# Memory attention of an encoder block: transposing the probabilities by halves of 64 query rows, into a PSUM tile of two banks

## The chip, the cores and the metric

The kernel runs on one core of a Trainium2 chip. The metric is the device time of one execution in microseconds (us). The kernel before takes 1399.69 us, the median of three runs (1399.4 to 1401.97).

## The reference, cut to what matters

The program is one encoder block on `x` of 1024 tokens by 1024 channels, in float32. Three mixers (dilated window attention "a", grouped-query attention "b", cross-attention into a memory of 256 tokens "m") are computed from one normalised input, gated, projected and merged. The change lies in the third mixer:

```python
kvm = rms_norm(mem, g_mem[layer]) @ w_mem_kv[layer]
km = kvm[..., :M_Q].reshape(b, n_mem, M_HEADS, M_HEAD_DIM)      # 256 keys, 4 heads of 128
vm = kvm[..., M_Q:].reshape(b, n_mem, M_HEADS, M_HEAD_DIM)
sm = jnp.einsum('bshd,bnhd->bhsn', mq.reshape(b, s, M_HEADS, M_HEAD_DIM), km).astype(jnp.float32)
pm = jax.nn.softmax(sm * (M_HEAD_DIM ** -0.5), axis=-1).astype(dt)
om = jnp.einsum('bhsn,bnhd->bshd', pm, vm).reshape(b, s, M_Q)
```

So for each of 4 heads there is a 1024 x 256 matrix of probabilities `pm` (queries by keys), and a product of it with 256 x 128 values.

## The kernel before, in words

Most products are made in float32r: each operand is split into a high and a low part (`split`, lines 106 to 108: ScalarE copies the high part, VectorE subtracts it from the source), and three products high-high, high-low and low-high are summed in PSUM. The kernel walks through stages: a start with keys, values and the memory's projections; the memory attention, together with the queries of mixer "b"; the attention of "b"; the long projections of mixer "a"; its window attention; the merge and the output projection.

The stage of the change runs from about 100 to 217 us. Its TensorE work is written out in an order by hand: `weave` takes steps of two generators in turn. One gives dense work from a queue (`b_q`, lines 301 to 305, matmuls with 256 moving columns; `mq_unit` and `add_gate`, lines 145 to 149, matmuls with 512 moving columns). The other is `m_att(h)`, the attention of one memory head. The order of the other engines' instructions is chosen by a scheduler; TensorE keeps the written order. The calls at the end of the stage are one `weave(1)` with dense work alone (the first `b_q`), then two queue items woven with head 0, two with head 1, one with head 2 and one with head 3.

`m_att(h)` works through its 1024 queries in four groups n of 256, as two tiles j of 128 query rows. In one step of its loop come `scores(n)`, then `trans(n - 2)`, then `pv(n - 3)`:

- `scores` (lines 579 to 595): six matmuls (line 127) into one PSUM bank, the row minimum on VectorE (line 586), its scaling (587), two exponentials on ScalarE (589), a reciprocal (592) and two scalings on VectorE (594). The result is the tile `pm`: 128 query rows by 2 j by 256 keys.
- `trans` (lines 597 to 606): four TensorE transposes (line 602), one for each tile j of queries and each half kt of the keys. A transpose is a matmul whose loaded weights are a 128 x 128 block of `pm` and whose moving operand is the 128 x 128 identity `ident`, a slice of the tile `cs`; so the profile names it `tr<-cs,pm`. All four land in one PSUM bank `tr`, from `pst()`, of which there are two in turn. Then `split` makes `mph` (ScalarE, line 107) and `mpl` (VectorE, line 108) from it, and the bank is free for the next but one group when `mpl` has been made.
- `pv` (lines 608 to 617): six matmuls (line 127, `ov<-mph,vmh` and so on) from `mph`, `mpl` and the values into a PSUM bank `ov`, a copy on ScalarE (616) and a DMA.

PSUM has eight banks. Two, named `d`, belong to the dense work for the whole program. The other six are given to each stage by `phase_psum(name, s2, s1, t, o)`: `s2` tiles of two banks (`pss()`), `s1` tiles of one bank (`pss1()`), `t` tiles of one bank for transposes (`pst()`), and `o` tiles for outputs (`pso()`). The start and the memory attention share one such opening, `phase_psum("ps_m", s1=3, t=2, o=1)`. Then comes `ps_b` for the attention of "b". `late` is a list of left-over pieces of the start that use `pst()`; `mq_unit` and `add_kv` take from it.

Some stages far behind the change run TensorE on parts of its 128 x 128 array, which the profile shows as rows*columns behind the operands' names: `64*128` (line 1589, scores of mixer "a" with a head dimension of 64: two heads, one on rows 0 to 63 and one on rows 64 to 127, into different banks), `64*64` (lines 1582 and 1654) and `128*64` (lines 821 and 1661). These are float32 matmuls, and the trace has two rows for each of them in the program. The transposes have one row each.

Of the kernel before, what the change touches and what calls it, by code (L numbers as in the profile page):

```python
# [50 lines left out]
def block(ctx: ExitStack, tc: tile.TileContext, x, xT, memT, cst, msk, bcst, tabA, gpost,  # L51
          wu, wv, wb, wmem, wbr, wout, out):
    nc = tc.nc
    V, A, G, PE = nc.vector, nc.scalar, nc.gpsimd, nc.tensor
# [12 lines left out]
    def phase_psum(name, s2=0, s1=0, t=0, o=0):  # L67
        assert 2 * s2 + s1 + t + o <= 6
        bank["n"] = (s2, s1, t, o)
        bank["i"] = 0  # L70
        bank["pool"] = tc.tile_pool(name=name, bufs=1, space=bass.MemoryType.PSUM, reuse_waits="tile")
        bank["p"] = bank["pool"].__enter__()

    def end_psum():
        bank["pool"].__exit__(None, None, None)

    def pss():
        return bank["p"].tile([P, 2, 512], F32, name="sc", tag="s2", bufs=bank["n"][0])

    def pss1():  # L80
        return bank["p"].tile([P, 512], F32, name="s1", tag="s1", bufs=bank["n"][1])

    def pst():
        bank["i"] += 1
        return bank["p"].tile([P, 4, 128], F32, name="tr", tag="t", bufs=bank["n"][2])

    def pso():
        return bank["p"].tile([P, 512], F32, name="ov", tag="o", bufs=bank["n"][3])
# [5 lines left out]
    ident = cs[:, C_ID:C_ID + 128]  # L94
# [11 lines left out]
    def split(dst_h, dst_l, src):  # L106
        A.activation(dst_h, src, AF.Copy)  # L107
        V.tensor_tensor(dst_l, src, dst_h.bitcast(F32), op=OP.subtract)  # L108
# [3 lines left out]
    def load_w(src, n=1024):  # L112
        if extra:
            extra.append(extra.pop(0))
        raw = (extra[0] if extra else wp).tile([P, 1024], F32, name="wr", bufs=WR)
        nc.sync.dma_start(raw[:, :n], src)
        wh = wp.tile([P, 1024], R, name="wh")
        wl = wp.tile([P, 1024], R, name="wl")
        split(wh[:, :n], wl[:, :n], raw[:, :n])
        k = n // 128  # L120
        return (wh[:, :n].rearrange("p (k f) -> p k f", k=k),
                wl[:, :n].rearrange("p (k f) -> p k f", k=k))

    def passes(out_ps, terms):
        n = len(terms)
        for i, (a, b) in enumerate(terms):
            PE.matmul(out_ps, a, b, start=i == 0, stop=i == n - 1)
# [37 lines left out]
    def run_items(count):  # L165
        for _ in range(count):
            n = done[0]
            prepare(n)
            prepare(n + 1)
            yield from queue[n][1](ready.pop(n))  # L170
            done[0] += 1

    def cost_items(count):
        return sum(q[2] for q in queue[done[0]:done[0] + count])
# [3 lines left out]
    def weave(count, att=None, att_cost=0.0, lead=1.0, prio=ATT_PRIO):  # L178
        dg = run_items(count)
        dc = cost_items(count)  # L180
        d = a = 0.0
        steps = 0
        live_d, live_a = True, att is not None
        while live_d or live_a:
            if live_d and (not live_a or a / att_cost >= min(1.0, d / dc * lead)):
                try:
                    d += next(dg)
                    steps += 1
                    if pend and steps % pace[0] == 0:
                        pend.pop(0)()  # L190
                except StopIteration:
                    live_d = False
                    d = 1e18
            else:
                try:
                    with tc.high_priority(offset=prio):
                        a += next(att)
                except StopIteration:
                    live_a = False
# [128 lines left out]
    kt = []  # L328
# [18 lines left out]
    late = []  # L347
# [102 lines left out]
    for k in range(8):  # L450
        if k % 2 == 0:
            load_wkv(k // 2)
        for e in range(2 if k == 0 else 1):
            t = slice(e * 512, e * 512 + 512) if k == 0 else slice(0, S)
# [29 lines left out]
    for c in range(2):  # L484
        t = st.tile([P, 4, 256], F32, name=f"mt{c}", tag=f"xk{c}")
# [86 lines left out]
    def m_att(h):  # L572
        qh, ql = MQ[h]
        for _ in range(4):
            yield 250
        st = {}

        def scores(n):
            sv = pss1().rearrange("p (t k) -> p t k", t=2)
            nm = mt_.tile([P, 2], F32, name="mnm", bufs=3)  # L580
            l = mt_.tile([P, 2], F32, name="mls", bufs=3)
            pm = mt_.tile([P, 2, 256], F32, name="pm", bufs=2)
            for j in range(2):
                t = slice((2 * n + j) * 128, (2 * n + j) * 128 + 128)
                passes(sv[:, j], [(qh[:, t], kmh[:, h]), (qh[:, t], kml[:, h]), (ql[:, t], kmh[:, h])])
            V.tensor_reduce(nm, sv, axis=AX.X, op=OP.min)
            V.tensor_tensor(nm, nm, rcol[:, 2 * n:2 * n + 2], op=OP.mult)
            for j in range(2):
                A.activation(pm[:, j], sv[:, j], AF.Exp, scale=nrcol[:, 2 * n + j:2 * n + j + 1], bias=nm[:, j:j + 1],
                             accum_out=l[:, j:j + 1])  # L590
            rl = mt_.tile([P, 2], F32, name="mrl", bufs=4)
            V.reciprocal(rl, l)
            for j in range(2):
                fp["mv"] = V.tensor_scalar(pm[:, j], pm[:, j], rl[:, j:j + 1], None, op0=OP.mult)
            st[n] = pm

        def trans(n):
            pm = st[n]
            tp = pst().rearrange("p (k t) q -> p k t q", k=2)
            for kt in range(2):  # L600
                for j in range(2):
                    PE.transpose(tp[:, kt, j, :], pm[:, j, kt * 128:kt * 128 + 128], ident)
            ph = mt_.tile([P, 2, 256], R, name="mph", bufs=2)
            pl = mt_.tile([P, 2, 256], R, name="mpl", bufs=2)
            split(ph, pl, tp.rearrange("p k t q -> p k (t q)"))
            st[n] = (ph, pl)

        def pv(n):
            ph, pl = st.pop(n)
            o = pso()  # L610
            terms = []
            for kt in range(2):
                terms += [(vmh[:, kt, h], ph[:, kt]), (vmh[:, kt, h], pl[:, kt]), (vml[:, kt, h], ph[:, kt])]
            passes(o[:, 0:256], terms)
            om = mt_.tile([P, 256], F32, name="om", bufs=2)
            A.activation(om, o[:, 0:256], AF.Copy)
            nc.sync.dma_start(od[2, h, :, n * 256:n * 256 + 256], om)

        for n in range(7):
            if n < 4:  # L620
                scores(n)
            yield 654
            if 0 <= n - 2 < 4:
                trans(n - 2)
            yield 436
            if 0 <= n - 3 < 4:
                pv(n - 3)
            yield 654
# [45 lines left out]
    add_gate(2, 2)  # L674
    early[len(queue)] = lambda: load_w(wu[U_G + 11])
    weave(1)
    weave(2, m_att(0), M_COST, 1.2)
    weave(2, m_att(1), M_COST, 1.2)
    weave(1, m_att(2), M_COST, 1.0)
# [548 lines left out]
    for n in range(28):  # L1228
        i, k = divmod(n, 4)
# [17 lines left out]
        for stage in (2, 1, 0):  # L1247
            r, at = divmod(n - 6 - (0, 2, 3)[stage], 3)
# [28 lines left out]
    for n in range(28):  # L1277
        i, k = divmod(n, 4)
# [5 lines left out]
        for j in range(4):  # L1284
            c = slice(j * 128, j * 128 + 128)
# [187 lines left out]
    r = RV[last, 0, 1]  # L1473
# [595 lines left out]
    s1 = [t[:, x] for t in [wp.tile([P, 1024], F32, name="wr", bufs=WR) for _ in range(2)] for x in half]  # L2069
# [127 lines left out]
    q, r = ss[7], ss[7][:, 3:4]  # L2197
# [148 lines left out]
```

## Time and profile before

| what | value |
|---|---|
| median of three runs | 1399.69 us (1399.4 to 1401.97) |
| the profiled execution, its own time | 1401.0 us |
| its span, from the first to the last instruction | 1399.2 us |
| mean granted TensorE clock | 0.997 |
| busy: TensorE, VectorE, ScalarE, GpSimd | 98%, 73%, 47%, 41% of the span |

"PE" is TensorE's matmuls, "PEld" its weight loads, DVE is VectorE, ACT ScalarE, POOL GpSimd, SP the engine that issues DMAs. In a timeline each row gives the start in us, the time in us, engine, line, operation, output tile and operand tiles, TensorE rows*columns, the shape of the moving operand and the number of instructions merged into the row. A matmul's time runs until its results are out, so the times of successive matmuls overlap; how fast they follow each other is read from the starts.

### The profile page before, as it was taken

To read this page: it belongs to the slowest core of one execution; us is meant where nothing else is said; L and a number is where in the kernel's file an instruction comes from. 1 tells how busy PE (TensorE), PEld (TensorE's weight loads), DVE (VectorE), ACT (ScalarE), POOL (GpSimd) and SP (SyncE) were. 2 spreads that over 40 slices of the span, in tenths; PEclk is the share of its full clock that TensorE was granted. 3 is DMA by queue.
4 is the path that set the end of the run, shared out by engine and by line. 5 is a ranking of instruction groups with operands and counts; after the bars stand their busy time and mean duration, and the time that the engine had idled before them with its cause. 6 is when DMAs were issued, how large, how long until landed. Compare 5 with 4: busy or idle time off the path is not lost.

```text
span 1399.2 us, 21844 instructions
## 1 busy us (share of the span) xinstructions
PE 1375.7 (98%) x7775; PEld 1105.8 (79%) x7775; DVE 1019.9 (73%) x1824; ACT 658.5 (47%) x1384; POOL 579.9 (41%) x444
## 2 busy tenths in 40 slices
PE   7999999999999999999999999999999999999997
PEld 7799986666666789988888888888887787778886
DVE  7768667776776597776777776677776566668977
ACT  6544455656655345333333333333336666653332
POOL 0507702675666000245555554355651243552003
PEclk9999999999999999999999999999999999999999
DMA  6356522322243688424323333333337676876455
GB/s 233 105 181 209 187 102 98 102 83 84 80 142 127 221 258 253 139 83 134 98 93 106 120 112 114 106 121 119 114 121 266 193 197 191 254 189 214 147 193 180
DMA packets 121933, 212.30 MB, mean 152 GB/s; under 512 B 32512, under 2 KB 61024, under 8 KB 121824
## 3 DMA queue, kind: packets, MB, share of 16 engines
q1 hardware_dynamic: 112512, 196.98, 44.0%
q10 hardware_dynamic: 9312, 13.93, 2.7%
q8 instruction: 61, 1.00, 0.3%
q14 instruction: 48, 0.39, 0.1%
HBM read 144.48 MB, written 66.38 MB: 151 GB/s over the span
## 4 chain that ended last, share of the span: by engine, by line
PE 89%; DVE 3%; POOL 2%; DMA 2%; ACT 2%; issue 1%; SPq 0%; DVEq 0%; POOLq 0%; ACTq 0%
PE s L1326 35%; PE d L1891 6%; PE s L1236 4%; PE s L2115 4%; PE ov L821 3%; PE sc L2033 3%; PE s L1287 3%; PE d L147 3%; PE d L145 3%; PE d L149 3%; PE s L1589 2%; PE tr L1661 2%; PE tr L787 2%; PE s L806 2%; PE s L805 2%; PE d L2115 2%
## 5 line engine op out<-in xcount | busy, mean ns | idle before, releaser
L812 POOL TENSOR_TENSOR bl<-bl,bp 128x512 f32<-128x512 f32 x96 | 133.1, 1386 | 54.2 <-ACT bp L808 48.7
L1326 PE MATMUL s<-hh,vS 128*128 128x512 f32 x400 | 133.4, 395 | 0.0
L1326 PE MATMUL s<-vA,vS 128*128 128x512 f32 x450 | 106.6, 390 | 0.0
L108 DVE TENSOR_TENSOR vS<-vot,vS 128x512 fp32r<-128x512 f32 x75 | 86.4, 1153 | 19.9 <-ACT vS L107 19.9
L1601 DVE CUSTOM_DVE_ANT_0 pra<-s,mask 128x192 f32<-128x192 f32 (+2 forms) x192 | 52.8, 327 | 63.8 <-PE s L1589 35.9
L1326 PEld LDWEIGHTS s<-vA,vS 128*128 128x128 f32 x450 | 84.5, 188 | 18.3
L808 ACT ACTIVATE bp<-s 128x512 f32<-128x512 f32 x128 | 75.6, 595 | 43.3 <-PE s L806 42.3
L788 DVE TENSOR_REDUCE bn<-tr 128x1 f32<-128x512 f32 x128 | 84.9, 683 | 12.9 <-PE tr L787 11.7
L145 PE MATMUL d<-hh,wh 128*128 128x512 f32 x224 | 89.3, 399 | 2.4 <-DVE fth L218 2.4
L1602 ACT ACTIVATE pra<-pra,sts 128x192 f32<-128x192 f32 (+2 forms) x176 | 75.2, 430 | 31.5 <-DVE sts L1601 31.4
L149 PE MATMUL d<-hh,wl 128*128 128x512 f32 x224 | 89.4, 399 | 0.0
L1326 PEld LDWEIGHTS s<-hh,vS 128*128 128x128 f32 x400 | 75.3, 188 | 17.7
L147 PE MATMUL d<-hl,wh 128*128 128x512 f32 x224 | 88.8, 397 | 0.0
L1326 PE MATMUL s<-hl,vS 128*128 128x512 f32 x200 | 79.1, 395 | 0.0
L1326 PE MATMUL s<-hh,wh 128*128 128x512 f32 x200 | 78.4, 392 | 0.0
L1326 PE MATMUL s<-hh,wl 128*128 128x512 f32 x200 | 78.4, 392 | 0.0
L1326 PE MATMUL s<-hl,wh 128*128 128x512 f32 x200 | 77.8, 389 | 0.0
L1330 ACT ACTIVATE vv<-s 128x512 f32<-128x512 f32 x50 | 29.9, 598 | 85.8 <-PE s L1326 59.3
L1070 POOL TENSOR_TENSOR vot<-wr 128x512 f32<-128x512 f32 x13 | 22.2, 1707 | 111.7 <-DVE vv L1206 111.7
L821 PE MATMUL ov<-bp,VS 128*64 128x512 f32 x256 | 58.5, 599 | 0.0
L1070 POOL TENSOR_TENSOR vot<-vot,vA 128x512 f32<-128x512 f32 x12 | 19.3, 1608 | 90.8 <-DVE vS L108 90.8
L145 PEld LDWEIGHTS d<-hh,wh 128*128 128x128 f32 x224 | 42.2, 188 | 16.2 <-issue 5.5
(629 smaller groups left out, 4050.9 us busy)
## 6 DMA issues: line engine op xcount, KB each, us to landing
wr<-in_wu SPq DMA_DIRECT2D x40, 512.0 KB
vA<-in_wu SPq DMA_DIRECT2D x24, 512.0 KB
qkd<-ko SPq DMA_DIRECT2D x96, 128.0 KB
wl<-thd SPq DMA_DIRECT2D x24, 512.0 KB
wos<-os SPq DMA_DIRECT2D x12, 512.0 KB
wr<-in_wbr SPq DMA_DIRECT2D x24, 256.0 KB
aq<-qkd SPq DMA_DIRECT2D x12, 512.0 KB
ak<-qkd SPq DMA_DIRECT2D x12, 512.0 KB
```

Source lines behind the costliest of these rows:

```text
L108: V.tensor_tensor(dst_l, src, dst_h.bitcast(F32), op=OP.subtract)
L145: PE.matmul(dst, wh[:, k, :], hh[k][:, t], start=k == 0, stop=False)
L147: PE.matmul(dst, wh[:, k, :], hl[k][:, t], start=False, stop=False)
L149: PE.matmul(dst, wl[:, k, :], hh[k][:, t], start=False, stop=k == 7)
L788: fp["last"] = V.tensor_reduce(st[i]["n"][:, j, c:c + 1], s, axis=AX.X, op=OP.min)
L808: A.activation(pp, s, AF.Exp, scale=-1.0)
L812: G.tensor_tensor(lsum[i % 2], lsum[i % 2], pp, op=OP.add)
L821: PE.matmul(o[e * 64:e * 64 + 64], VS[:, kt, kv], d.pop(kt), start=kt < 2, stop=kt >= NT - 2)
L1326: PE.matmul(BANK[n, c], a, b, start=k == 0 and q == 0 and not more, stop=k == 3 and q == 2, skip_group_check=c in "XW")
L1602: A.activation(src, src, AF.Exp, scale=-1.0, bias=bias, accum_out=sts[:, 1, h, T:T + 1])
L1891: PE.matmul(ps_, a, b, start=k == 0 and q == 0, stop=k == 3 and q == 2)
L2115: PE.matmul(dst[:, e[0]:e[1]], a, b, start=k == 0 and q == 0, stop=k == 3 and q == 2)
```

## The change

`trans` takes a tile of two banks from `pss()` in place of one bank from `pst()`. Each of the four transposes becomes two: one of query rows 0 to 63 (r = 0, rows 0 to 63 of TensorE, into the first bank) and one of query rows 64 to 127 (r = 1, rows 64 to 127, into the second bank), each with 64 x 128 probabilities as weights and a 64 x 64 identity as the moving operand. `split` reads the two banks in one instruction each and writes `mph` and `mpl` in the same order as before. For this the stage's PSUM is opened anew behind the first dense item: `ps_h` has one tile of two banks, three tiles `s1` and one tile `o`, six banks in all.

```diff
         def trans(n):
             pm = st[n]
-            tp = pst().rearrange("p (k t) q -> p k t q", k=2)
+            tp = pss()
             for kt in range(2):
                 for j in range(2):
-                    PE.transpose(tp[:, kt, j, :], pm[:, j, kt * 128:kt * 128 + 128], ident)
+                    for r in range(2):
+                        rs, c = slice(64 * r, 64 * r + 64), 128 * kt + 64 * j
+                        PE.transpose(tp[:, r, c:c + 64], pm[rs, j, kt * 128:kt * 128 + 128], ident[rs, rs])
             ph = mt_.tile([P, 2, 256], R, name="mph", bufs=2)
             pl = mt_.tile([P, 2, 256], R, name="mpl", bufs=2)
-            split(ph, pl, tp.rearrange("p k t q -> p k (t q)"))
+            split(*[z.rearrange("p k (t r q) -> p r (k t) q", t=2, r=2) for z in (ph, pl)],
+                  tp[:, :, 0:256].rearrange("p r (m q) -> p r m q", m=4))
             st[n] = (ph, pl)
@@
     early[len(queue)] = lambda: load_w(wu[U_G + 11])
     weave(1)
+    assert not late
+    end_psum()
+    phase_psum("ps_h", s2=1, s1=3, o=1)
     weave(2, m_att(0), M_COST, 1.2)
```

The transposes' line is 602 before and 604 after; later lines move by 3, and by 6 behind the new opening. There are now eight transposes in each of 16 groups (4 heads by 4 groups), and one tile for them in place of two in turn. On TensorE the order of everything else is as before. On VectorE and ScalarE the built program holds the same instructions, and for head 2 in a slightly other order; the DMA issues of that stage change places in a few spots.

## The prediction

> **What bounds the kernel now.** I read the page's busy shares first, then the stretch that holds the change, then its list of waits.
>
> ```profile
> PE 1375.7 (98%) x7775; PEld 1105.8 (79%) x7775; DVE 1019.9 (73%) x1824; ACT 658.5 (47%) x1384; POOL 579.9 (41%) x444
> PE 89%; DVE 3%; POOL 2%; DMA 2%; ACT 2%; issue 1%; SPq 0%; DVEq 0%; POOLq 0%; ACTq 0%
> ```
>
> TensorE is busy 98% of the span and makes 89% of the chain that ended last.
>
> ```profile
> 100.00:217.00 117.00, 117.00 (x817) 108.19 (x816) 83.72 (x203) 56.90 (x139) 54.08 (x81) 1.00 0.47 163
> ```
>
> This is the stage of the change: length, then busy time of TensorE, its weight loads, VectorE, ScalarE, GpSimd, then clock, DMA share and GB/s. TensorE works 117.00 of 117.00 us. In the list of waits from 100 to 240 us only one line is TensorE's, and it lies in the next stage:
>
> ```profile
> PE tr L787 <- DVE bn L788: 0.5, 1, 0.5
> ```
>
> So what the change adds to or takes from TensorE's sequence moves the end nearly one to one; what it does to the other engines counts only where TensorE comes to wait.
>
> **The transposes now.** Two groups in TensorE's timeline, the first among 256-column matmuls, the second among 512-column ones:
>
> ```profile
> 124.47 0.28 PE L303 MATMUL d<-wbh,hl 128*128 128x256 f32 x1
> 124.59 0.60 PE L602 MATMUL tr<-cs,pm 128*128 128x128 f32 x4
> 124.94 0.36 PE L305 MATMUL d<-wbl,hh 128*128 128x256 f32 x1
> 125.14 0.28 PE L301 MATMUL d<-wbh,hh 128*128 128x256 f32 x1
> 125.26 0.28 PE L303 MATMUL d<-wbh,hl 128*128 128x256 f32 x1
> ...
> 184.96 0.39 PE L145 MATMUL d<-hh,wh 128*128 128x512 f32 x1
> 185.19 0.60 PE L602 MATMUL tr<-cs,pm 128*128 128x128 f32 x4
> 185.55 0.48 PE L147 MATMUL d<-hl,wh 128*128 128x512 f32 x1
> 185.86 0.39 PE L149 MATMUL d<-hh,wl 128*128 128x512 f32 x1
> ```
>
> From the group's start to the second dense matmul behind it: 125.14 - 124.59 = 0.55 and 185.86 - 185.19 = 0.67 us. One step of dense work is in it (125.26 - 125.14 = 0.12; 185.19 - 184.96 = 0.23), so four transposes cost 0.43 to 0.44 us, 0.11 each, with no gap on either side. All 16 groups are thus 16 x 0.44 = 7.0 us, and no change to them can win more.
>
> **What is removed and added on TensorE.** No row before shows a half transpose in a series, so its price comes from other work on parts of the array, late in the kernel:
>
> ```profile
> 1068.81 0.40 PE L1891 MATMUL d<-hh,wh 128*128 128x512 f32 x1
> 1069.13 1.14 PE L1589 MATMUL s<-ak,aq 64*128 64x256 f32 x8
> 1070.20 0.50 PE L1891 MATMUL d<-hh,wh 128*128 128x512 f32 x1
> 1070.54 0.40 PE L1891 MATMUL d<-hl,wh 128*128 128x512 f32 x1
> 1070.78 0.40 PE L1891 MATMUL d<-hh,wh 128*128 128x512 f32 x1
> ...
> 1097.89 0.46 PE L1582 MATMUL s<-ak,aq 64*64 64x64 f32 x16
> 1098.28 0.76 PE L1628 MATMUL tr<-cs,pra 128*128 128x128 f32 x5
> ...
> 1109.83 1.15 PE L1654 MATMUL tr<-app,avs 64*64 64x64 f32 x32
> 1110.91 1.03 PE L1589 MATMUL s<-ak,aq 64*128 64x128 f32 x9
> ```
>
> Three things are read here.
>
> *Parts work side by side.* Line 1654 issues 32 matmuls of 64 moving columns, two at a time on different rows: 16 sets take 1110.91 - 1109.83 = 1.08 us. Line 1582 issues 16, four at a time: 4 sets take 0.39. If a set costs c and going in and out costs d, 16c + d = 1.08 and 4c + d = 0.39, so c = 0.058 and d = 0.16 us. Eight half transposes are four such sets: 4 x 0.058 + 0.16 = 0.39 us until the next dense matmul may start.
>
> *Going in costs.* Line 1589 starts 0.32 us behind a 512-column matmul that is followed after 0.24 otherwise (1070.78 - 1070.54): 0.08 to 0.09 us in which the array runs empty.
>
> *Coming out costs beyond d.* The first dense matmul behind takes until 1070.54 - 1070.20 = 0.34 in place of 0.24: 0.10 us, its weight load, which otherwise hides behind the matmul ahead.
>
> The Trainium skill, TensorEngine Tiling (Array Packing), Key Properties, says that changing the tiling mode, not just the tile, drains TensorE. The rows above agree (0.08 us on the way in). The Trainium skill's Theoretical Speedup on the same page gives up to 2x for a dimension of 64 or less; by that alone, an estimate, the 7.0 us would become 3.5.
>
> Sum for one group among 512-column work: 0.09 in + 0.39 + 0.34 = 0.82 us to the second dense matmul behind, against 0.67 now: +0.15. Among 256-column work the dense steps are 0.12 on both sides, so it is the same. 16 groups: +2.4 us.
>
> The weights of a half transpose are 128 columns wide, those of line 1654 64. Their loads:
>
> ```profile
> L602 PEld LDWEIGHTS tr<-cs,pm x64: 137/140/143, 110.3 to 211.9; 128*128 128x128 f32 x64
> L1654 PEld LDWEIGHTS tr<-app,avs x256: 129/135/228, 1109.8 to 1257.9; 64*64 64x64 f32 x128
> ```
>
> 140 against 135 ns, so I take c as it stands. One single half transpose is in the trace, with the very shape:
>
> ```profile
> 1252.77 0.24 PE L1929 MATMUL s<-cs,rows 64*128 64x64 f32 x1 [1.82 <-DMA rows<-std]
> 1252.95 0.50 PE L1891 MATMUL d<-bh,wh 128*128 128x512 f32 x1
> 1253.28 0.40 PE L1891 MATMUL d<-bl,wh 128*128 128x512 f32 x1
> ```
>
> Start to next start is 0.18, where c + d says 0.22; with 0.04 less a group costs +0.11 and all 16 +1.8 us. The 0.33 behind it confirms the exposed load. I take +0.14 a group, **+2.2 us**, with 1.8 to 2.4 from these rows. The outer ends: if the two halves did not run side by side, eight steps of 0.058 in place of four add 0.23 a group, +6.0 us in all; if going in and out cost nothing, 4 x 0.058 = 0.23 replaces 0.44, -3.3 us.
>
> **One tile in place of two.** A group's transposes now wait until `mpl` of the group before is made, which two banks made needless. Behind a waiting transpose stands all dense work of TensorE. `mph` and `mpl` still take one instruction each of the same 512 elements (598 and 684 ns):
>
> ```profile
> L107 ACT ACTIVATE mph<-tr x16: 587/598/608, 112.2 to 212.4; 128x512 fp32r<-128x512 f32 x16
> L108 DVE TENSOR_TENSOR mpl<-tr,mph x16: 673/684/692, 113.8 to 213.0; 128x512 fp32r<-128x512 f32 x16
> ```
>
> The two tightest places of before:
>
> ```profile
> 119.27 0.68 DVE L108 TENSOR_TENSOR mpl<-tr,mph 128x512 fp32r<-128x512 f32 x1
> 119.95 0.60 PE L602 MATMUL tr<-cs,pm 128*128 128x128 f32 x4
> ...
> 189.21 0.59 ACT L107 ACTIVATE mph<-tr 128x512 fp32r<-128x512 f32 x1
> 189.69 0.56 ACT L589 ACTIVATE pm<-s,mnm,nrcol 128x256 f32<-128x256 f32 x1
> 189.83 0.69 DVE L108 TENSOR_TENSOR mpl<-tr,mph 128x512 fp32r<-128x512 f32 x1 [0.22 <-ACT mph L107]
> 190.13 0.21 ACT L589 ACTIVATION_READ_ACCUMULATOR pm<-s,mnm,nrcol 128x1 f32 x1
> 190.44 0.16 DVE L592 RECIPROCAL mrl<-mls 128x2 f32<-128x2 f32 x1
> 190.49 0.60 PE L602 MATMUL tr<-cs,pm 128*128 128x128 f32 x4
> 190.63 0.62 DVE L594 TENSOR_SCALAR pm<-pm,mrl 128x256 f32<-128x256 f32 x2
> ```
>
> At the first, `mpl` ends at 119.95, just when the next group starts; going in delays that start by 0.09, and this covers the signal. At the second (head 2) the built program's order changes: the second exponential comes ahead of `mph` on ScalarE, and the reciprocal and the two scalings ahead of `mpl` on VectorE. Then `mph` runs about when the exponential ran, to 190.3; the scalings end about 0.5 us earlier than their 191.25, near 190.7; `mpl` ends near 191.4, with one group's lateness (0.14) 191.5. TensorE gets there at 190.49 + 2 x 0.14 + 0.09 = 190.86, so it waits some **0.5 us** (0 if the exponentials come earlier, 0.7 at most by these rows). The other groups have 0.2 us or more, and lateness of TensorE helps them. Nothing else waits for it: `pv` of that group follows 0.7 us behind the transposes.
>
> **The rest at nothing.** The new opening of PSUM stands where only dense items have run; its tiles wait for readers some microseconds old, and TensorE's bank `d` covers that (if not: one evacuation, 0.6 us). The few DMAs of head outputs that change places are read hundreds of microseconds later.
>
> **Sum.** 2.2 + 0.5 = +2.7 us on the profiled execution's 1401.0 (span 1399.2 and 1.8 around it): 1403.7. The median of the runs shown stands 1.3 lower, so I predict **1402.4 us**.
>
> **Rivals.**
>
> *The halves run one after the other* (+6.0 + 0.5: 1406.2). For it: no transposes are seen side by side. Against it: line 1589 on the same rows*columns makes eight matmuls of 256 columns in 1.07 us, and the single half transpose looks like any other of 64 columns.
>
> *No drain between transposes and dense work: faster.* It acts at both ends of each of the 16 groups. For it: transposes of 128 rows join dense matmuls without a gap. Price: 7.0 us become 16 x 0.23 = 3.7, so -3.3: 1396.4. It decides when in and out together cost under 0.2 us a group; the rows say 0.35. The Trainium skill's Theoretical Speedup (TensorEngine Tiling (Array Packing)) is this case.
>
> *Drain, but hidden loads.* Without the first load (0.05) and the exposed one (0.10) a group costs about 0.44 as now: no change but the one wait, 1400.2. The 0.33 and 0.34 behind part-array work speak against it.
>
> *The single tile binds everywhere*: 12 groups have a follower in their head; 0.6 us each is +7, with 2.2 some 1409. Against it stand the slacks above.
>
> **How the numbers follow.** Forecast 0.62, one after the other 0.15, no drain 0.07, hidden loads 0.12, single tile 0.04. About 0.2% (2.8 us) is what a measurement of this kernel can tell from no change. My forecast of +2.7 sits on that bound, with 1.8 to 3.1 as its own range, so it gives just under half of its chance to slower; with the first and last rivals that is 0.48. Faster is the no-drain case, 0.07; 0.45 remains for no change. The range 1400.0 to 1406.2 leaves out the no-drain and single-tile cases.
>
> **What would show it.** Behind: groups of eight `64*128` transposes, starting 0.3 us behind a 512-column matmul, about 0.39 us to the next start, and a first dense matmul that takes 0.1 us longer to its follower. From 100 us to the first transposes of line 712 (215.9 before) about 2.7 us more. In the waits, one of TensorE for `mpl` in head 2. Wrong: starts at the usual rhythm on either side (no drain), a group of 0.6 us or more (no overlap), waits for `mpl` in most groups, or a difference that arises behind this stage.

## The result and the profile after

| | before | changed |
|---|---|---|
| median (9 runs each) | 1399.4 us (1397.92 to 1401.97) | 1403.5 us (1401.1 to 1404.7) |
| ratio, 95% interval | | 1.0029 (1.002 to 1.0038): +4.1 us (2.8 to 5.3) |
| profiled execution, span | 1399.2 us | 1402.9 us |
| mean granted clock | 0.997 | 0.997 |

The change made the kernel slower, as predicted, and by somewhat more than the predicted +2.7 us (1402.4), which lies just under the interval. The busy shares of the page after say no more than before: TensorE still holds the span.

```profile
PE 1379.1 (98%) x7839; PEld 1104.3 (79%) x7839; DVE 1020.7 (73%) x1824; ACT 658.4 (47%) x1384; POOL 580.6 (41%) x444
```

64 matmuls more (128 half transposes for 64 whole ones). The stage by itself can be measured between two landmarks that no version touches: the first score matmul of the memory attention and the first transposing matmul of the next stage. The rows are of the views by line and by tile of before (first two) and after; behind the durations stand the first and the last start.

```profile
L127 PE MATMUL s<-kmh,mqh x32: 276/282/385, 99.4 to 205.4; 128*128 128x256 f32 x32
L787 PE MATMUL tr<-KS,QH x21: 388/393/500, 218.9 to 239.1; 128*128 128x512 f32 x21
```

```profile
L127 PE MATMUL s<-kmh,mqh x32: 276/280/333, 100.1 to 209.0; 128*128 128x256 f32 x32
L793 PE MATMUL tr<-KS,QH x18: 390/396/497, 222.8 to 239.9; 128*128 128x512 f32 x18
```

The stage took 218.9 - 99.4 = 119.5 us and takes 222.8 - 100.1 = 122.7: **+3.2 us**. This "stage" is the measure for all experiments below, since it doesn't see what varies elsewhere from run to run. It is read from one profile of each run, and differs by up to 0.3 us from what the groups of transposes show by themselves (e2, e3).

The same two places as in the prediction, in TensorE's timeline of after, one among 256-column and one among 512-column matmuls:

```profile
125.59 0.28 PE L301 MATMUL d<-wbh,hh 128*128 128x256 f32 x1
125.70 0.28 PE L303 MATMUL d<-wbh,hl 128*128 128x256 f32 x1
125.91 0.46 PE L604 MATMUL sc<-cs,pm 64*128 64x64 f32 x8
126.30 0.38 PE L305 MATMUL d<-wbl,hh 128*128 128x256 f32 x1
126.52 0.28 PE L301 MATMUL d<-wbh,hh 128*128 128x256 f32 x1
...
187.03 0.40 PE L145 MATMUL d<-hh,wh 128*128 128x512 f32 x1
187.36 0.46 PE L604 MATMUL sc<-cs,pm 64*128 64x64 f32 x8
187.75 0.50 PE L147 MATMUL d<-hl,wh 128*128 128x512 f32 x1
188.09 0.39 PE L149 MATMUL d<-hh,wl 128*128 128x512 f32 x1
188.32 0.40 PE L145 MATMUL d<-hh,wh 128*128 128x512 f32 x1
```

Read the starts. On the way in 125.91 - 125.70 = 0.21 us, where the usual step of dense work is 125.70 - 125.59 = 0.11 to 0.12. In the group 126.30 - 125.91 = 0.39. On the way out 126.52 - 126.30 = 0.22 in place of 0.12. From the last dense start to the second dense start behind: 126.52 - 125.70 = 0.82 us; before it was 125.14 - 124.47 = 0.67. So +0.15 for the group. At 187 us 188.09 - 187.03 = 1.06 against 185.86 - 184.96 = 0.90: +0.16. Over the 16 groups the difference is 0.13 to 0.16 us in 15 and 0.90 in one, together 3.17: the whole +3.2 of the stage.

The one is the third group of head 2. The stretch from 100 to 220 us (its length, then TensorE's busy time), and TensorE's only wait there in the list of waits (time in all, times, longest):

```profile
100.00:220.00 120.00, 119.33 (x880) 106.79 (x880) 83.24 (x203) 56.12 (x138) 54.62 (x81) 1.00 0.45 160
```

```profile
PE sc L604 <- DVE mpl L108: 0.7, 1, 0.7
```

The timeline of all engines there, from the group before (rows of other work left out):

```profile
190.29 0.46 PE L604 MATMUL sc<-cs,pm 64*128 64x64 f32 x8
...
190.68 0.19 PEld L149 LDWEIGHTS d<-hh,wl 128*128 128x128 f32 x1
190.68 0.50 PE L149 MATMUL d<-hh,wl 128*128 128x512 f32 x1
...
190.85 0.56 ACT L589 ACTIVATE pm<-s,mnm,nrcol 128x256 f32<-128x256 f32 x1 [0.26 <-PE sc L604]
...
191.40 0.55 ACT L589 ACTIVATE pm<-s,mnm,nrcol 128x256 f32<-128x256 f32 x1
...
191.94 0.59 ACT L107 ACTIVATE mph<-sc 128x512 fp32r<-128x512 f32 x1
...
192.35 0.62 DVE L594 TENSOR_SCALAR pm<-pm,mrl 128x256 f32<-128x256 f32 x2
...
192.41 0.19 PEld L147 LDWEIGHTS d<-hl,wh 128*128 128x128 f32 x1
...
192.64 0.40 PE L147 MATMUL d<-hl,wh 128*128 128x512 f32 x1
...
192.88 0.68 DVE L108 TENSOR_TENSOR mpl<-sc,mph 128x512 fp32r<-128x512 f32 x1
...
193.71 0.46 PE L604 MATMUL sc<-cs,pm 64*128 64x64 f32 x8 [0.67 <-DVE mpl L108]
```

The transposes are done at about 190.7, but ScalarE makes two exponentials before it makes `mph`, VectorE two scalings before `mpl`, and TensorE, whose last dense matmul started at 192.64, may use the one tile only at 193.71: 0.67 us without work.

The two rows of weight loads show the way out. Among 512-column work the load of a matmul starts about 0.23 us ahead of it, beside the matmul before (192.41 for the one at 192.64). Behind the halves load and matmul both start at 190.68, so the load isn't hidden there.

### The profile page after: what moved, and what is told of

The parts are those of the page before. It is cut to its first block, busy times and chain, and to the rows that moved or that the text cites. A ratio compares the mean times of both kernels' runs of the same rounds, so it can differ in the third digit from the quotient of the medians.

```text
span 1402.9 us, 21969 instructions
## 1 busy us (share of the span) xinstructions
PE 1379.1 (98%) x7839; PEld 1104.3 (79%) x7839; DVE 1020.7 (73%) x1824; ACT 658.4 (47%) x1384; POOL 580.6 (41%) x444
## 4 chain that ended last, share of the span: by engine, by line
PE 57%; DMA 1%; DVE 1%; SPq 0%; issue 0%; ACT 0%; DVEq 0%; ACTq 0%
PE s L1332 34%; PE d L1897 6%; PE s L2121 4%; PE sc L2039 3%; PE tr L1667 2%; PE s L1595 2%; PE d L2121 2%; PE tr L1634 1%; PE s L1293 1%; PE tr L1660 1%; PE tr L1643 0%; PE s L1588 0%; PE tr L1619 0%; DMA ak<-qkd 0%; DMA tab<-in_tabA 0%; DMA avs<-vdr 0%
## 6 DMA issues: line engine op xcount, KB each, us to landing
qkd<-ko SPq DMA_DIRECT2D x96, 128.0 KB
```

## The experiments

Theory: the loss is the price of a visit. Going from work on the whole array to work on row halves and back costs some 0.35 us, more than the halves win by running side by side, and one wait for `mpl` comes on top. Rivals: the halves don't run side by side, or are dear in themselves; the one tile in place of two makes the loss; the new opening of PSUM does. The table has each run's stage by the same two landmarks and its ratio to the kernel before.

| run | stage, us | against before | ratio (95%) |
|---|---|---|---|
| before | 119.5 | | |
| changed | 122.7 | +3.2 | 1.0029 (1.002 to 1.0038) |
| e1_reopen | 119.6 | +0.1 | 1.0002 (0.9994 to 1.0011) |
| e2_whole_one_tile | 120.1 | +0.6 | 1.0004 (0.9995 to 1.0014) |
| e3_halves_serial | 123.1 | +3.6 | 1.0031 (1.002 to 1.0043) |
| e4_halves_split_first | 122.6 | +3.1 | 1.0029 (1.0019 to 1.0038) |
| e5_two_visits | 128.0 | +8.5 | 1.0062 (1.0047 to 1.0077) |
| e6_pair_visits | 125.5 | +6.0 | 1.0037 (1.0023 to 1.0051) |
| e7_same_rows | 126.5 | +7.0 | 1.0053 (1.0036 to 1.007) |
| e8_whole_plus_two | 126.3 | +6.8 | 1.0053 (1.0038 to 1.0069) |
| e9_pair_spread | 120.9 | +1.4 | 1.002 (1.0011 to 1.003) |
| e10_pair_split_first | 120.8 | +1.3 | 1.0019 (1.001 to 1.0028) |
| e11_changed_again | 122.6 | +3.1 | 1.0028 (1.0018 to 1.0038) |

**e1: the kernel before, with the PSUM opened anew** (same tiles).

```diff
+    assert not late
+    end_psum()
+    phase_psum("ps_h", s1=3, t=2, o=1)
```

> The kernel before with its PSUM opened anew at the same place, but in the old shape (three single banks, two for transposes, one for outputs) and with whole transposes. My theory (array switches 16 x 0.15 us, and one wait for the single tile): nothing, 0 +- 1 us, the transposes' groups as before. Rival, the new opening itself costs: +1 us or more, with a wait of TensorE behind the first dense item.

Stage +0.1 us, time the same, and no wait of TensorE in the stage: the new opening by itself costs nothing that shows.

**e2: whole transposes into one tile of two banks** (the changed kernel's PSUM).

```diff
-                    for r in range(2):
-                        rs, c = slice(64 * r, 64 * r + 64), 128 * kt + 64 * j
-                        PE.transpose(tp[:, r, c:c + 64], pm[rs, j, kt * 128:kt * 128 + 128], ident[rs, rs])
+                    PE.transpose(tp[:, kt, j * 128:j * 128 + 128], pm[:, j, kt * 128:kt * 128 + 128], ident)
```

> Whole 128 x 128 transposes, but into the one tile of two banks, with the PSUM opened as after the change. My theory: no array switch, so the 16 x 0.15 us vanish; on VectorE the built order has mpl of the tenth group right behind the scalings of the group before, as in the kernel before, so the wait is 0 to 0.2 us: +0 to +0.5 us in all. Rival, the single tile is most of the loss: +1 to +4 us, with waits for mpl in several groups.

Stage +0.6 us, of which the starts show 0.33 at the groups (two waits of 0.13 and 0.18 us), time the same by its interval. The other 0.3 lie in no one place. So one tile alone costs a few tenths, and the other 2.6 us come with the halves. In e2 VectorE also makes `mpl` ahead of the next scalings, as in before, so that the long wait of after doesn't arise.

**e3: all halves of rows 0 to 63 first, then those of rows 64 to 127.**

```diff
-            for kt in range(2):
-                for j in range(2):
-                    for r in range(2):
+            for r in range(2):
+                for kt in range(2):
+                    for j in range(2):
```

> The changed kernel with the four transposes of rows 0 to 63 first and then the four of rows 64 to 127. My theory: a set's 0.06 us is one weight load with one stream, and neighbours on the same rows can't overlap, so a group takes 7 to 8 steps of 0.06 in place of 4 and costs 0.2 us more: 16 x 0.2 = +3.2 us beyond the changed kernel, about +7 us against before. Rival, halves don't overlap in the changed kernel either: the same time as the changed kernel, about +4 us.

This expectation failed: the stage is only 0.4 us longer than the changed kernel's. A group in TensorE's timeline:

```profile
110.22 0.28 PE L301 MATMUL d<-wbh,hh 128*128 128x256 f32 x1
110.42 0.47 PE L604 MATMUL sc<-cs,pm 64*128 64x64 f32 x8
110.83 0.39 PE L303 MATMUL d<-wbh,hl 128*128 128x256 f32 x1
```

0.41 us from the group's start to the next dense one (0.40 unrounded), 0.01 to 0.02 more than in after. Either nothing runs side by side and a half takes 0.03 us, or TensorE starts the halves of the other rows although three are issued ahead of them. e7 tells these apart.

**e7: all eight halves on rows 0 to 63.**

```diff
-                        PE.transpose(tp[:, r, c:c + 64], pm[rs, j, kt * 128:kt * 128 + 128], ident[rs, rs])
+                        PE.transpose(tp[:, r, c:c + 64], pm[0:64, j, kt * 128:kt * 128 + 128], ident[0:64, 0:64])
```

> The changed kernel with all eight half transposes of a group on query rows 0 to 63: those of rows 64 to 127 are replaced by a repetition of the ones of rows 0 to 63, so the output is wrong in the memory attention. Number, shape, tiles and order of the instructions stay. Theory (halves on different rows work side by side, a half alone would take a whole step of 0.06 us): four more steps of 0.06 us in each of 16 groups, +3.8 us beyond the changed kernel, some 1407, and 0.63 us from the start of a group to the next dense matmul in place of 0.39. Rival (a half transpose simply takes 0.03 us, whatever its rows, and nothing works side by side): the same time as the changed kernel, some 1403, and 0.39 to 0.40 us a group.

```profile
110.46 0.28 PE L301 MATMUL d<-wbh,hh 128*128 128x256 f32 x1
110.67 0.71 PE L604 MATMUL sc<-cs,pm 64*128 64x64 f32 x8
111.31 0.39 PE L303 MATMUL d<-wbh,hl 128*128 128x256 f32 x1
111.53 0.28 PE L305 MATMUL d<-wbl,hh 128*128 128x256 f32 x1
```

111.31 - 110.67 = 0.64 us, 0.25 more than in after: four more steps of 0.06. Stage +7.0, 3.8 beyond the changed kernel, as the theory said. (This kernel leaves out the transposes of rows 64 to 127 of each tile.) Halves of different rows do run side by side, and e3 shows that they need not be issued in turn.

**e5: each group's eight halves in two visits of four.**

```diff
-        def trans(n):
+        def trans(n, kt):
...
-                trans(n - 2)
-            yield 436
+                trans(n - 2, 0)
+            yield 218
+            if 0 <= n - 2 < 4:
+                trans(n - 2, 1)
+            yield 218
```

> The changed kernel with each group's eight half transposes in two visits of four (one half of the keys each), with dense matmuls between: the same instructions, twice the switches. My theory: a visit costs 0.35 us for going in and out whatever it holds, so 16 more visits add 16 x 0.35 = +5.6 us to the changed kernel: about +9 us against before. Rival, the loss lies in the half transposes themselves (slower streams, more instructions): no more than 1 us beyond the changed kernel.

The same halves, and 5.3 us more in the stage than the changed kernel (128.0 - 122.7), of which 0.3 is a new wait of TensorE of 1.0 for a bank of scores in place of the 0.7 for `mpl`. The edit doesn't part every group: in the second groups of heads 2 and 3 no dense matmul comes between, and the eight halves stay together. So there are 30 visits, 14 more and not 16, at 5.0 / 14 = 0.36 us each. One of a group's two visits:

```profile
110.66 0.28 PE L301 MATMUL d<-wbh,hh 128*128 128x256 f32 x1
110.87 0.34 PE L606 MATMUL sc<-cs,pm 64*128 64x64 f32 x4
111.14 0.39 PE L303 MATMUL d<-wbh,hl 128*128 128x256 f32 x1
111.36 0.28 PE L305 MATMUL d<-wbl,hh 128*128 128x256 f32 x1
```

Four halves take 0.27 us where eight take 0.39: two steps of 0.06 less, while the 0.21 on the way in and the 0.22 on the way out stay.

**e8: whole transposes, and ahead of them one half of each row half** (into columns that nobody reads).

```diff
             tp = pss()
+            for r in range(2):
+                rs = slice(64 * r, 64 * r + 64)
+                PE.transpose(tp[:, r, 448:512], pm[rs, 0, 0:128], ident[rs, rs])
```

> The kernel with whole transposes into one tile of two banks (which took the time of the kernel before), and ahead of the four whole ones of each group one half transpose of each row half into columns of the tile that nobody reads. Theory (going into and out of work on half the rows costs about 0.35 us a visit, a pair of halves 0.06): 16 x 0.36 to 0.41 = +5.8 to +6.6 us, some 1405 to 1406, with 0.2 us ahead of the first half. Rival (the loss of the changed kernel is in the halves themselves, (7.0 + 2.4) / 128 = 0.073 us each): 32 x 0.073 = +2.3 us, some 1401.7.

One pair of 0.06 us a group costs 6.2 us in the stage beyond e2 (126.3 - 120.1), 0.9 of it a wait for `mpl`, so 5.3 / 16 = 0.33 a group, or 0.35 since the 0.3 us of small waits of e2 are gone. The price of a visit by itself:

```profile
110.92 0.28 PE L301 MATMUL d<-wbh,hh 128*128 128x256 f32 x1
111.13 0.28 PE L602 MATMUL sc<-cs,pm 64*128 64x64 f32 x2
111.34 0.66 PE L605 MATMUL sc<-cs,pm 128*128 128x128 f32 x4
111.75 0.36 PE L303 MATMUL d<-wbh,hl 128*128 128x256 f32 x1
111.95 0.28 PE L305 MATMUL d<-wbl,hh 128*128 128x256 f32 x1
```

111.95 - 110.92 = 1.03 us against 0.67 in before: +0.36, of which one step is 0.06. The visit is 0.30 here: 0.09 in, and the rest between the pair and the first dense matmul, where the whole transposes wait and their first one is slow. The rival (+2.3) falls: these 32 halves cost more than twice what the 128 of the changed kernel do.

**e4: `mph` and `mpl` ahead in the order of ScalarE and VectorE.**

```diff
-            split(*[z.rearrange("p k (t r q) -> p r (k t) q", t=2, r=2) for z in (ph, pl)],
-                  tp[:, :, 0:256].rearrange("p r (m q) -> p r m q", m=4))
+            with tc.high_priority(offset=400):
+                split(*[z.rearrange("p k (t r q) -> p r (k t) q", t=2, r=2) for z in (ph, pl)],
+                      tp[:, :, 0:256].rearrange("p r (m q) -> p r m q", m=4))
```

> The changed kernel with a higher priority for the two parts mph and mpl, which puts mpl of the tenth group ahead of the next reciprocal and scalings again. My theory: the switches stay, 15 to 16 groups at +0.15 us = +2.4, and the wait of 0.74 us before the eleventh group goes to 0.1 or less: +2.4 us against before. Rival, the wait comes from the single tile whatever the order: it stays above 0.5 us there or comes up in another group, +3 us or more.

```profile
PE s L127 <- ACT pm L589: 0.5, 1, 0.5
```

The wait for `mpl` is gone, as expected, and the 16 groups together are down to +2.4 us, each +0.13 to +0.16. The total missed: the exponentials are later, TensorE waits for a bank of scores instead, and the stage gains only 0.1 us. With one tile, the wait of after is thus owed to the order of two engines, and putting one pair first puts the other last.

**e6, e9, e10: two groups of halves in one visit**, to save half of the visits; e9 moves the two products with v of a pair apart, e10 adds e4's order to e9. The core of it (e9 and e10 then place `pv(n - 4)` and `pv(n - 3)` 1.1 us of planned work apart):

```diff
-            pm = mt_.tile([P, 2, 256], F32, name="pm", bufs=2)
+            pm = mt_.tile([P, 2, 256], F32, name="pm", bufs=3)
...
-            tp = pss()
+            if n % 2 == 0:
+                st["tp"] = pss()
+            tp = st["tp"][:, :, 256 * (n % 2):256 * (n % 2) + 256]
...
+            if n in (3, 5):
+                for f in (trans, parts):
+                    for g in (n - 3, n - 2):
+                        f(g)
...
+            if n in (4, 6):
+                for g in (n - 4, n - 3):
+                    pv(g)
```

> Two groups' half transposes in one visit of sixteen, which fills the two banks (a third buffer of probabilities, the products with the values a step later): half the switches. My theory: a visit costs 0.35 + 8 x 0.06 = 0.83 us against 2 x 0.44 = 0.88 for the whole transposes of before: 8 x -0.05 = -0.4 us in the visits, and some waits, since probabilities and parts have less time: -0.4 to +1.5 us against before. Rival, the loss is by half transpose: +2.4 us or more.

> As the kernel with the half transposes of two groups in one visit, but the two products with v of a pair stand 1.1 us of planned work apart, so that the second doesn't wait for the single bank of its output. Theory (the price is by the visit, and what that kernel lost beyond it were those waits of 3.9 us): eight switches fewer than in the changed kernel, 8 x 0.35 = 2.8 us less than its +2.4 without the wait for mpl, so -0.4 us against the kernel before, up to +1.0 if one or two new waits come, and no wait for the output's bank over 0.2 us. Rival (half transposes are dear by themselves): +2.4 or more.

> As the run with two groups in one visit and the products with v apart, whose stage was 1.4 us longer than that of before, of which the trace gives 1.4 us to two waits that came with the new order (0.8 for the probabilities of head 2 and 0.6 for mpl ahead of a product with v): here mph and mpl are put ahead in the order of ScalarE and VectorE. Theory (price by the visit): without waits the stage is 0.3 us shorter than that of before, with the waits that stay 0 to +0.8 us, and the time in the runs -0.5 to +1.5. Rival (half transposes lose by themselves, however many share a visit): the stage stays at +1.4 or more where no wait of TensorE is left.

All three missed on the total, and the times of e6 and e9 are what the rival gave (+2.4 or more). The rows of single visits tell the two apart. e6 met eight waits for the single bank of `pv`'s output:

```profile
PE ov L127 <- ACT om L625: 3.9, 8, 0.5
```

e9 removed them, and shows what a pair costs:

```profile
112.59 0.28 PE L303 MATMUL s<-wbh,hl 128*128 128x256 f32 x1
112.80 0.71 PE L606 MATMUL sc<-cs,pm 64*128 64x64 f32 x16
113.44 0.39 PE L127 MATMUL s<-kmh,mqh 128*128 128x256 f32 x1
113.67 0.28 PE L127 MATMUL s<-kml,mqh 128*128 128x256 f32 x1
```

Sixteen halves take 0.64 us, and the whole visit 113.67 - 112.59 = 1.08, of which two dense steps of 0.12 are dense work: 0.84 for two groups, where whole transposes take 2 x 0.43 to 0.44 = 0.86 to 0.88. So the price by the visit holds, and at two groups halves and whole transposes are level. The total is not: heads 2 and 3 meet new waits, by the starts 1.3 us in e9 (0.7 for probabilities not yet scaled in the later pair of head 2, 0.6 for `mpl` ahead of a product with v) and 1.1 us in e10 (0.7 and 0.4 in the later pairs of both heads). The list of waits has only 0.3 for each of the first three and nothing for the last, since it counts no time in which an earlier matmul still runs. Without these waits the stage would be 0.1 to 0.2 us longer than before's, not 0.3 shorter as the theory gave. Their timed +2.8 us (1.5 to 4.2) and +2.7 (1.4 to 3.9) reach down to the stage's +1.4 and +1.3; what lies above is not explained. No version that beats the kernel before came out of this.

**e11: the changed kernel once more.**

> The changed kernel itself, beside the kernel before on the same chip, since its timed difference (+4.1 us, 2.8 to 5.3) and the growth of its stage in the trace (+3.2) stand 0.9 apart. Theory (all of it lies in the stage): the stage again 3.1 to 3.4 us longer, the time +2.5 to +4.0. Rival (a further microsecond is lost behind the stage, by work that moved with it): the time +4 or more, and the distance from the stage's end to the end of the span longer by 1 us than in the kernels whose stage took no longer.

Stage +3.1 us, time +3.9 (2.5 to 5.3), and the same single wait of 0.7 us for `mpl`. From the stage's end (221.8) to the end of the span (1401.8) it is 1180.0 us, in before 1399.2 - 218.9 = 1180.3, so nothing is lost there in this pair. The rival stays open all the same. That distance differs by more than the microsecond in question between single profiles (1178.4 to 1183.8, see the last section), and in nine of the ten runs with halves the timed difference lies above the stage's, by 0.2 to 1.4 us. Nearly all of this lies within the intervals, and several runs share the same runs of before, so it shows no loss; but it excludes none either.

## Why the prediction was right

- *TensorE bounds the stage, so what is added to it goes one to one.* Right: the groups' 3.17 us are the stage's 3.2.
- *Parts work side by side, a set costs 0.058 us.* Right: e7's four extra steps cost 0.25 us, 0.06 each. The 0.058 was read from lines 1654 and 1582, on tiles of 64*64, and carried to 64*128; that it holds there was assumed, and e5 (two steps less, 0.12 us) and e7 show it. The rival "one after the other" priced +6.5 us in all; e7, which forces it, has +7.0.
- *Going in costs 0.08 to 0.09, in and out together 0.16, and the weight load behind another 0.10.* Right: 0.09 in, 0.39 - 4 x 0.06 = 0.15, and 0.10 behind, 0.34 a visit; e5 gives 0.36 for one visit more and e8 0.30 towards transposes of 128 rows. The rival of no drain falls with the 0.21 in place of 0.12, that of hidden loads with the 0.22 in place of 0.12 and the load at 190.68.
- *+0.14 a group, +2.2 us.* The mechanism right, the term a little small: 0.13 to 0.16, 2.4 us over 16. The prediction took a middle between 0.15 from two series and 0.11 from the one single half transpose of the trace; the series was the nearer relative.
- *One tile in place of two, a wait of 0.5 us at the third group of head 2.* Right in place and cause, too small: 0.67 by the record of waits, 0.74 by the starts (193.71 - 192.64 = 1.07 where 0.33 is usual). Two steps were short. The prediction's own figures, 191.5 for the end of `mpl` and 190.86 for TensorE, are 0.64 apart and not 0.5; in after `mpl` ended at 192.88 + 0.68 = 193.56, 0.59 behind the moment when TensorE was ready (192.64 + 0.33 = 192.97). And the prediction let the transposes start when `mpl` ends; they started at 193.71, 0.15 later. At its other tight place, at 119 us before, `mpl` ends 0.5 us ahead of the transposes in after (120.60 and 121.12), so it's not shown that going in covers those 0.15. The other groups didn't wait, as forecast, and e2 has no large wait either, so "binds everywhere" falls.
- *PSUM opened anew and DMAs moved: nothing.* Right for the opening (e1). The DMAs were not tried alone; no row of TensorE in the stage waits for one.
- *The sum.* +2.7 forecast, +3.2 in the stage: 0.2 more from the groups and 0.24 from the wait. The timed +4.1 and +3.9 have the stage's 3.2 in their intervals (2.8 to 5.3, 2.5 to 5.3). The 0.8 to 0.9 above it are not explained. The prediction named a difference that arises behind this stage as a sign of being wrong; whether there is one, no run here settles.

The rule of the Trainium skill, TensorEngine Tiling (Array Packing), Key Properties, that a change of tiling mode drains TensorE, agrees with the 0.09 us on the way in. The Theoretical Speedup on the same page of the Trainium skill (up to 2x) is nearly reached inside a visit: a pair of halves does the work of one whole transpose in 0.06 us in place of 0.11. By that alone the stage would have gained; here eight instructions are too few for a visit of 0.34.

## What to carry to other kernels

Work on parts of the array was priced by the visit here: halves save about 0.05 us for each whole transpose replaced (0.11 - 0.06), a visit costs 0.30 to 0.36, so a visit needs some seven replaced transposes before it gains (eight were level here, with 0.03 us won). Before splitting work among dense matmuls, count the switches, not the instructions. And a version that bundles the visits has to be read for what the bundle makes late elsewhere: here each one gave its gain back in a wait for a single bank or for another engine's order.

## What was not expected of the hardware

*Halves of other rows seem to overtake.* In e3 four halves of rows 0 to 63 are issued ahead of four of rows 64 to 127, and the group takes 0.41 us, not the 0.64 of e7: the later ones run beside the earlier. The starts of single halves, which the rows above merge, agree: in e7 they come one by one, 0.06 us and more apart; in after and in e3 they come in pairs, 0.003 to 0.004 and 0.01 to 0.02 us apart, save in the group behind the wait. Which rows a record belongs to isn't in the trace, so it remains an inference from these times.

*A wait comes and another goes far behind the change.* Some 350 us later TensorE waits 0.8 us in after where it doesn't in before, behind a DMA on which VectorE waits longer; the first row is of the list of waits of before, the next two of after:

```profile
DVE tab L1270 <- DMA tab<-in_tabA: 3.0, 1, 3.0
```

```profile
DVE tab L1276 <- DMA tab<-in_tabA: 4.5, 1, 4.5
PE s L1293 <- DVE wl L108: 0.8, 1, 0.8
```

And before has a wait of 1.8 us late in the kernel that after doesn't have (e1, e3, e6 and e7 have it too, with 1.6 to 2.1):

```profile
PE s L1929 <- DMA rows<-std: 1.8, 1, 1.8
```

The order of the instructions there is the same in both kernels. VectorE's wait for `tab` is 2.8 to 3.0 us in before, e1, e2 and e8, 3.5 in e6, and 4.0 to 5.8 in the other eight profiles of halves; TensorE waits at that line in those eight alone. Why it is longer there, with e8 (halves too, and as late) among the short ones, stays open. This 0.8 us may be part of what the timed differences have above the stage's; that isn't shown. All this is the reason for measuring a change of 3 us by its stage: from the stage's end to the end of the span it is 1180.3 us in before, 1178.4 in e2 (1397.5 - 219.1) and 1183.8 in e10 (1404.2 - 220.4).
